# A two-layer hybrid diffusion step on one core: loads unpinned early, normalisation interleaved with gate products, attention paced closer

## The chip, the core and the metric

The kernel runs on one core of a Trainium2 chip. Its engines work side by side, each through a list of its own: TensorE (PE) multiplies matrices, VectorE (DVE), ScalarE (ACT) and GpSimd (POOL) do the elementwise work, and SyncE (SP) issues nearly all the transfers. A wait at the head of an engine's list holds back everything behind it on that engine. The metric is the device time of one execution in microseconds (us); lower is better.

## What is computed

The reference runs two layers. In each, 1024 latent tokens and 256 context tokens of width 1024 are normalised and modulated, go through one wide input projection, then through three token mixers (A, B and C), which are gated, merged and projected back:

```python
def mixer_inputs(x, cond, norm_g, w_ada, b_ada, w_in):
    mod = jax.nn.silu(cond) @ w_ada + b_ada
    ...
    shift, scale, gate = jnp.split(mod, 3, axis=-1)
    h = rms_norm(x, norm_g) * (1 + scale) + shift
    return jnp.split(h @ w_in, IN_OFFSETS, axis=-1), gate

def latent_layer(x, c, ka_c, va_c, kb_c, vb_c, st, ...):
    (aq, ak, av, ag, bq, bk, bv, bg, cx, cg, ga, gb, gc), gate = mixer_inputs(x, c, norm_g, w_ada, b_ada, w_in)
    ...
    ya = window_attention(qa, ka, va, ka_c, va_c, a_sink) * jax.nn.silu(ag)
    yb = neighbourhood_attention(qb, kb, vb, kb_c, vb_c, b_rpb) * jax.nn.silu(bg)
    ...
    yc = (hf + hb).astype(x.dtype) * jax.nn.silu(cg)
    out = merge_branches(ya, yb, yc, ga, gb, gc, w_br, w_out)
    return x + gate * out
```

The columns `ga`, `gb`, `gc` (1024 each) and `ag`, `bg`, `cg` (512 each) of the projection are gates: nothing needs them before the merge at the end of the layer. Mixer C is a linear recurrence over the tokens, behind a small convolution of `cx`. A and B are softmax attentions with 8 heads each; a latent query sees 512 cached keys and two or three blocks of 128 local ones.

## The kernel before

**Tiles.** Tokens stand in three chunks: 0 and 1 are the latent tokens (512 each), 2 is the context (256). Activations are kept as eight tiles of 128 features (k = 0 to 7), each split into a high and a low part (`hhl`/`hll` for the latent tokens, `hhc`/`hlc` for the context), and so are the weights. A product (`job`) makes 128 output columns of one chunk: 8 values of k with three matmuls each, high by high, low by high and high by low, so 24 matmuls of 512 or 256 columns.

**Weights.** `load_w` (L410) loads a job's weights in two halves into `wr` (two buffers); ACT casts each half to its high part (`wh`, four buffers), POOL subtracts for the low part (`wl`, four buffers). One job is loaded ahead of the one that runs (`Weave.fetch`, L137).

**The order.** The order on PE is written out by the program. `Weave` keeps a clock of its own, which each matmul advances, and two queues of jobs: `need` (what attention or the recurrence wait for) and `spare` (mostly the gates). Attention proceeds when its due times are reached, and a piece of a job (three matmuls) is put in wherever nothing is due. The other engines' lists come from a scheduler, which may move instructions by its own estimate. `ordered` (L210) holds the loads through it in program order while the list `starting` is not empty:

```python
def ordered(ins):
    return tc.keep_in_program_order(ins) if starting else ins
```

It is called on the loads of tokens (L1331), of weights (L414, L512), of the modulation (L1405) and on `keep` (L1355), which writes the transposed input to DRAM as `x_d`. A gate's way out is a copy on ACT into a tile `tgt` (L710) and a transfer from it into `g_d` (L711); these are not held.

**The first phase** (L1392 to L1471). Chunk 0 is transposed and normalised, then the gates of its columns 0 to 7 are made, then chunks 1 and 2 are transposed and their sums of squares taken. `fill(n)` puts in n pieces of gate jobs. `token_rstd` (two steps) makes the factors, and `norm_apply` normalises: per k a product on DVE (`nt`), an addition with a cast on ACT (`hhl`, L566) and a difference on DVE (`hll`, L567). The tiles `nt` and `tgt` share one tag, `g2`, with three buffers. In the traces `gt` is a gate product; in the order of instructions `gt_0_70` is the product for gate column 7 on chunk 0, and `wgt_0_70` its weights. After it comes `cx_0`, the first product of mixer C, on chunks 0, 1 and 2.

**Attention** (`chain`, L1079). A layer has 40 groups of 256 queries, in two steps each; a step scores two parts of 128 queries and one head (`sc` against the cached keys, `sl` against the local ones, both in PSUM tiles of tag `s`, of which there are two), and turns the probabilities of the step two before it (`pt`, `PT`) and multiplies them by the values (`o`). For one part DVE takes the minimum of `sc` (L981) and of both (L997), and ACT takes the exponentials (`P`, L1003 and L1005). A step starts no earlier than `pace` after the one before, on the clock of `Weave`, in ns:

```python
for s in range(2):
    yield max(g.q_at, g.keys.at["K"], paced)
    paced = W.now + T["pace"]
    yield from step(i, s, behind.popleft() if len(behind) == BEHIND else None)
```

The gate products that are left when attention ends run in the merge phase behind it. `sg` are the gate products of the mixers' own gates, the last in `spare`.

Of the kernel before, what the change touches and what calls it, by code (L numbers as in the profile page):

```python
# [76 lines left out]
PSB = {"d": 2, "s": 2, "t": 3, "o": 1}  # L77
LGB = ("s", "t")
LDB = ("d", "t")
T = dict(f1=9, f2=2, kc=10000, c0=10000, cq=1, gx=3, nx=8000, yo=1500, yi=1000, aq=9000, ac=7000, ms=2000, v=3200, tok=8600, scale=1100, t0=3400, tb=2200, o=2200, soft=7600, pace=9400, lg=320, lr=8500, cv=16000, le=4200)  # L80


class Weave:
# [107 lines left out]
def trunk(nc, tc, ctx, I, K, O):  # L191
# [20 lines left out]
    starting = [True]  # L212
# [28 lines left out]
    fill = cp.tile([P, 2], F32, name="fill")  # L241
# [304 lines left out]
    def sum_squares(l, ci, xs, acc, add):  # L546
        for k in range(KD):
            add_square(l, ci, k, xs[k][:, :CHUNKS[ci][1]], acc, add)
# [10 lines left out]
    def norm_apply(l, ci, xs, rs, H, ks=range(KD)):  # L559
        c0, N = CHUNKS[ci]  # L560
        cond = 0 if c0 < NLAT else 1
        for k in ks:
            t = cp.tile([P, 512], F32, tag="g2", name=f"nt{l}_{ci}_{k}", bufs=3)
            nc.vector.scalar_tensor_tensor(t[:, :N], xs[k][:, :N], hcol(l, k, cond), rs[:, :N], ALU.mult, ALU.mult)
            hh, hl = H.at(k, ci)
            nc.scalar.activation(hh, t[:, :N], AF.Identity, bias=scol(l, k, cond))  # L566
            nc.vector.scalar_tensor_tensor(hl, t[:, :N], scol(l, k, cond), f32(hh), ALU.add, ALU.subtract)  # L567
        W.mark(("H", l, ci), 6000)
# [813 lines left out]
    def fill(n):  # L1382
        for _ in range(n):
            W.dense()

    with tc.manual_schedule(engines={mybir.EngineType.PE}):
        sides = ("left", "right")
        hcm = pool("h0", side=sides[0])
        H = Hidden(hcm.__enter__(), 0)
        W.banks = ("d", "t")  # L1390
        jobs = gate_jobs(0, H)
        with pool("start", side=sides[1]) as sp:  # L1392
# [61 lines left out]
            xs.append(input_chunk(2, tk, sp))  # L1454
            acc.append(sp.tile([P, 512], F32, tag="nacc", name="nacc0_2", bufs=2))
            sum_squares(0, 2, xs[2], acc[2], nc.vector.tensor_add)
            fill(T["f1"])
            token_rstd(0, 1, acc[1])
            fill(T["f2"])
            token_rstd(0, 2, acc[2], "t", False)  # L1460
            norm_apply(0, 1, xs[1], acc[1], H)
            norm_apply(0, 2, xs[2], acc[2], H)
            for ci in (1, 2):
                for k in range(KD):
                    fill(1)
                    keep(ci, xs[ci], (k,))
                fill(1)
                if ci == 1:
                    constants(0)
            starting.clear()  # L1470
            bias_tables()  # L1471
        W.spare.extend((always, j((1, 2))) for j in jobs[:8])
        for l in range(DEPTH):
# [65 lines left out]
```

## Time and profile before

| what | value |
|---|---|
| median of 3 runs | 3178.77 us (3177.68 to 3180.86) |
| the profiled execution, its own time | 3178.1 us |
| its span in the profile | 3176.3 us |
| PE busy | 3081.1 us, 97% of the span |
| DVE, ACT, POOL busy | 1780.8, 1706.3, 969.8 us (56%, 54%, 31%) |
| 0 to 335 us | first phase and recurrence, layer 0 |
| 395 to 1290 us | attention, layer 0 |
| 1290 to 1990 us | merge, output, and the first part of layer 1 |
| 1990 to 2835 us | attention, layer 1 |
| 2835 to 3176 us | merge and output, layer 1 |

The busy time of an engine is the time in which one of its instructions was on. A matmul's record is longer than the distance to the next one, since matmuls overlap: rows at 0.39 us stand 0.23 us apart. Idle time of PE is listed with what ended it. The granted clock is TensorE's, as a share of 2.4 GHz; it has two levels, so a value between 0.5 and 1 for a stretch is a mean of both.

### The profile page before, as it was taken

Reading aid. Unit: us, or ns where it says so; the run is one execution under the profiler, and the core shown is the slowest. Engines: PE = TensorE matmul, PEld = TensorE weight load, DVE = VectorE, ACT = ScalarE, POOL = GpSimd, SP = SyncE. Lnnn points to the kernel's source line nnn. Section 1 sums busy time; section 2 is a strip of 40 time slices with the busy share of each in tenths; the row PEclk is TensorE's granted clock in tenths of the full one; section 3 lists DMA queues with packets and bytes.
Section 4 is the critical chain, followed back from the end, with each engine's and each line's share of the span. In section 5 each row is a group of like instructions: output and inputs, shape, how many; then the busy total and the mean of one; then the engine's idle time right before and its main releaser. Section 6 shows DMA issues by size and latency. Waiting matters only on the chain.

```text
span 3176.3 us, 48114 instructions
## 1 busy us (share of the span) xinstructions
PE 3081.1 (97%) x17421; PEld 2627.0 (83%) x17421; DVE 1780.8 (56%) x3293; ACT 1706.3 (54%) x3591; POOL 969.8 (31%) x815
## 2 busy tenths in 40 slices
PE   7799999999999999999999999999999999989999
PEld 5677788888888888888888888888888888878887
DVE  5475356666666664455364554665675666555531
ACT  5478355565555555444346864555555555544422
POOL 3364312223222120245343442222241222002632
PEclk9899999999999999999999999999999999989999
DMA  7554555535533232663442236455544333237443
GB/s 266 157 170 154 150 147 152 151 105 165 158 110 93 86 101 70 228 207 112 143 152 71 74 105 176 111 144 146 147 134 145 103 102 95 82 110 243 161 152 102
DMA packets 447434, 435.03 MB, mean 137 GB/s; under 512 B 75120, under 2 KB 368604, under 8 KB 445916
## 3 DMA queue, kind: packets, MB, share of 16 engines
q1 hardware_dynamic: 441212, 414.92, 43.9%
q0 software_dynamic: 5664, 16.83, 1.6%
q8 instruction: 137, 2.24, 0.3%
q14 instruction: 101, 0.83, 0.1%
q10 hardware_dynamic: 320, 0.21, 0.0%
HBM read 298.12 MB, written 137.29 MB: 137 GB/s over the span
## 4 chain that ended last, share of the span: by engine, by line
PE 78%; DVE 9%; ACT 5%; issue 3%; POOL 2%; DMA 2%; SPq 1%; ACTq 0%; DVEq 0%; POOLq 0%
PE gt L218 17%; PE sg L218 10%; PE o L218 7%; PE q L218 6%; PE pt L225 6%; PE po L218 5%; PE br L218 5%; PE k L218 4%; PE sc L218 4%; PE v L218 3%; PE cx L218 3%; PE sl L218 3%; POOL acc L1242 1%; PE lg L218 1%; DVE lR L687 1%
## 5 line engine op out<-in xcount | busy, mean ns | idle before, releaser
L427 ACT CAST PT<-pt 128x512 fp32r<-128x512 f32 (+2 forms) x528 | 271.7, 536 | 337.5 <-PE pt L225 335.4
L428 DVE TENSOR_TENSOR PT<-pt,PT 128x512 fp32r<-128x512 f32 (+2 forms) x528 | 319.5, 621 | 100.5 <-ACT PT L427 99.0
L981 DVE TENSOR_REDUCE st<-sc 128x1 f32<-128x512 f32 x256 | 176.3, 689 | 298.7 <-PE sc L218 298.2
L218 PE MATMUL gt<-hhl,wgt_h 128*128 128x512 f32 x736 | 299.7, 407 | 18.0 <-ACT wgt_h L422 18.0
L218 PE MATMUL gt<-hll,wgt_h 128*128 128x512 f32 x736 | 290.1, 394 | 0.0
L218 PE MATMUL gt<-hhl,wgt_l 128*128 128x512 f32 x736 | 289.9, 394 | 0.1
L225 PE MATMUL pt<-cst,P 128*128 128x128 f32 x1856 | 274.0, 274 | 9.4 <-DVE PT L428 7.5
L423 POOL TENSOR_TENSOR wgt_l<-wgt_r,wgt_h 128x512 fp32r<-128x512 f32 x110 | 173.0, 1580 | 335.6 <-ACT wgt_h L422 292.5
L225 PEld LDWEIGHTS pt<-cst,P 128*128 128x128 f32 x1856 | 217.7, 141 | 18.2 <-DVE PT L428 9.4
L218 PE MATMUL po<-z,wpo_h 128*128 128x512 f32 (+1 forms) x768 | 212.5, 364 | 7.7 <-ACT z L427 4.5
L1003 ACT ACTIVATE P<-sc,st 128x512 f32<-128x512 f32 x256 | 175.3, 685 | 61.7 <-DVE st L997 61.4
L218 PE MATMUL br<-yl,wbr_h 128*128 128x512 f32 (+1 forms) x576 | 205.2, 356 | 0.8 <-DVE yl L428 0.8
L218 PE MATMUL br<-yh,wbr_h 128*128 128x512 f32 (+1 forms) x576 | 204.7, 355 | 0.0
L218 PE MATMUL br<-yh,wbr_l 128*128 128x512 f32 (+1 forms) x576 | 204.5, 355 | 0.0
L423 POOL TENSOR_TENSOR wsg_l<-wsg_r,wsg_h 128x512 fp32r<-128x512 f32 x48 | 63.7, 1332 | 402.2 <-ACT wsg_h L422 398.4
L218 PE MATMUL sc<-Kpast,Q 128*128 128x512 f32 x512 | 168.4, 410 | 17.0 <-ACT P L1003 16.4
L218 PE MATMUL o<-PT,Vpast 128*128 128x256 f32 x1024 | 177.3, 295 | 3.7 <-DVE Y L1066 3.1
L218 PEld LDWEIGHTS gt<-hhl,wgt_h 128*128 128x128 f32 x736 | 138.8, 189 | 49.0 <-ACT wgt_h L422 18.4
L1005 ACT ACTIVATE P<-sl,st 128x384 f32<-128x384 f32 (+1 forms) x320 | 170.9, 534 | 4.6 <-DVE st L993 4.4
L218 PEld LDWEIGHTS gt<-hhl,wgt_l 128*128 128x128 f32 x736 | 138.5, 188 | 33.4 <-POOL wgt_l L423 1.2
L218 PEld LDWEIGHTS po<-z,wpo_h 128*128 128x128 f32 x768 | 137.1, 192 | 32.6 <-ACT z L427 5.8
L218 PEld LDWEIGHTS gt<-hll,wgt_h 128*128 128x128 f32 x736 | 139.0, 189 | 25.2 <-issue 0.5
(350 smaller groups left out, 8521.4 us busy)
## 6 DMA issues: line engine op xcount, KB each, us to landing
Q<-q_d SPq DMA_DIRECT2D x160, 256.0 KB
gl<-g_d SPq DMA_DIRECT2D x48, 640.0 KB
wgt_r<-in_w_in_dram SPq DMA_DIRECT2D x110, 256.0 KB
g_d<-tgt SPq DMA_DIRECT2D x92, 256.0 KB
wa<-in_w_ada_dram POOLq DMA_DIRECT2D x64, 256.0 KB, 4.2
wpo_r<-in_w_out_dram SPq DMA_DIRECT2D x64, 256.0 KB
yg<-y_d SPq DMA_DIRECT2D x24, 640.0 KB
yr<-s_d SPq DMA_DIRECT2D x24, 640.0 KB
```

The source lines that it names most:

```text
L218: nc.tensor.matmul(out, a, b, start=start, stop=stop)
L225: nc.tensor.transpose(out, x, idn)
L423: nc.gpsimd.tensor_sub(lo, r, f32(hi))
L427: nc.scalar.copy(hi, x)
L428: nc.vector.tensor_sub(lo, x, f32(hi))
L687: nc.vector.tensor_tensor_scan(h, a, u, st if c0 < NLAT else 0.0, ALU.mult, ALU.add)
L981: nc.vector.tensor_reduce(cm, psc, AX.X, ALU.min)
L1003: nc.scalar.activation(pt[:, nl * P:(nl + 4) * P], psc, AF.Exp, bias=m, scale=-1.0, accum_out=sums[:, t, x, 1:2])
L1005: nc.scalar.activation(pt[:, :nl * P], loc, AF.Exp, bias=m, scale=-1.0, accum_out=sums[:, t, x, 0:1])
L1242: (nc.vector if b == 0 and k >= KD - 2 else nc.gpsimd).tensor_add(z, z, g)
```

## The change

Three edits. The list `starting` is cleared ahead of `fill(T["f1"])`, so the loads and the `x_d` writes that come later in the program are no longer held in order. `norm_apply` for chunks 1 and 2 is called tile by tile between pieces of gate products, and `constants(0)` and the two calls of `keep` come behind them; the number of pieces is the same, 29. The due time between attention steps goes from 9400 to 9000.

```diff
-T = dict(f1=9, f2=2, ..., soft=7600, pace=9400, lg=320, lr=8500, cv=16000, le=4200)
+T = dict(f1=9, f2=2, ..., soft=7600, pace=9000, lg=320, lr=8500, cv=16000, le=4200)
...
             sum_squares(0, 2, xs[2], acc[2], nc.vector.tensor_add)
+            starting.clear()
             fill(T["f1"])
             token_rstd(0, 1, acc[1])
             fill(T["f2"])
             token_rstd(0, 2, acc[2], "t", False)
-            norm_apply(0, 1, xs[1], acc[1], H)
-            norm_apply(0, 2, xs[2], acc[2], H)
             for ci in (1, 2):
                 for k in range(KD):
+                    norm_apply(0, ci, xs[ci], acc[ci], H, (k,))
                     fill(1)
-                    keep(ci, xs[ci], (k,))
-                fill(1)
-                if ci == 1:
-                    constants(0)
-            starting.clear()
+            constants(0)
+            keep(1, xs[1])
+            keep(2, xs[2])
+            fill(2)
             bias_tables()
```

On SP, in the first phase, the row that matters is `g_d_0_5`, the way out of gate product 5, against the loads of `wgt_0_70`. Before:

```order
L1355 DMA x_d_6_78<-xi_6_719 128x512
L711 DMA g_d_0_5_117<-tgt_0_50_0_1035 128x512
L1355 DMA x_d_7_79<-xi_7_726 128x512
L414 DMA wgt_0_70_r_1074<-in_w_in_dram 128x4x128
L414 DMA wgt_0_70_r_1080<-in_w_in_dram 128x4x128
```

After, from the first load of `wgt_0_70` on, and then (second block) the stretch in which `g_d_0_5` stands now:

```order
L414 DMA wgt_0_70_r_995<-in_w_in_dram 128x4x128
L1355 DMA x_d_4_76<-xi_4_705 128x512
L1355 DMA x_d_5_77<-xi_5_712 128x512
L711 DMA g_d_0_4_116<-tgt_0_40_0_889 128x512
L414 DMA wgt_0_70_r_1001<-in_w_in_dram 128x4x128
```

```order
L414 DMA wcx_0_r_1140<-in_w_in_dram 128x4x128
L276 DMA sink_1229<-in_a_sink_dram 128x8
L414 DMA wgt_0_01_r_1174<-in_w_in_dram 128x4x128
L414 DMA wgt_0_01_r_1180<-in_w_in_dram 128x4x128
L414 DMA wgt_0_11_r_1298<-in_w_in_dram 128x4x128
L711 DMA g_d_0_5_117<-tgt_0_50_0_980 128x512
```

The loads of `wgt_0_70` moved ahead of `g_d_0_5`, and those of the three jobs behind it (`wcx_0`, `wgt_0_01`, half of `wgt_0_11`) too.

On ACT, in the same place, the casts of `wgt_0_70`, the copy `tgt_0_50` and the normalisation (`hhl`, `hhc`) share one list. Before:

```order
L566 ACTIVATE hhc_6_997<-nt_2_6_995,mod_222 128x256
L710 COPY tgt_0_50_0_1035<-gt_0_50_0_914 128x512
L710 COPY tgt_0_60_0_1119<-gt_0_60_0_1086 128x512
L566 ACTIVATE hhc_7_1003<-nt_2_7_1001,mod_222 128x256
L422 CAST wgt_0_70_0_h<-wgt_0_70_r_1074 128x512
L422 CAST wgt_0_70_4_h<-wgt_0_70_r_1080 128x512
```

After:

```order
L422 CAST wgt_0_70_0_h<-wgt_0_70_r_995 128x512
L533 ACTIVATE nw_1_895<-nacc_1_407 128x512
L533 ACTIVATE nw_2_920<-nacc_2_829 128x256
L422 CAST wgt_0_70_4_h<-wgt_0_70_r_1001 128x512
L566 ACTIVATE hhl_0_230<-nt_1_0_927,mod_222 128x512
L566 ACTIVATE hhl_1_232<-nt_1_1_934,mod_222 128x512
L566 ACTIVATE hhl_2_234<-nt_1_2_941,mod_222 128x512
L422 CAST wcx_0_0_h<-wcx_0_r_1134 128x512
```

The casts of `wgt_0_70` moved from behind the normalisation of chunks 1 and 2 to ahead of it, and those of `wcx_0` into it.

On PE, in attention, the pieces of gate products between two scores become fewer. This is the end of the first step of a group in layer 0 (the first group of the second head pair); `sc_1_0_1` is the first score of its second step. Before:

```order
L218 MATMUL gt_1_50_1_5007<-hhl_4_238,wgt_1_50_4_l 128x512
L218 MATMUL o_0_6_5025<-PT_0_6_0_2_5035,Vlat_0_3766 128x256 x4
L218 MATMUL o_0_6_5025<-PT_0_6_0_3_5044,Vlat_0_3766 128x128 x2
L218 MATMUL gt_1_50_1_5007<-hhl_5_240,wgt_1_50_4_h 128x512
L218 MATMUL gt_1_50_1_5007<-hll_5_241,wgt_1_50_4_h 128x512
L218 MATMUL gt_1_50_1_5007<-hhl_5_240,wgt_1_50_4_l 128x512
L218 MATMUL sc_1_0_1_5066<-Kpast_1_4885,Q_1_0_4666 128x512 x2
```

After:

```order
L218 MATMUL gt_1_50_1_5007<-hll_5_241,wgt_1_50_4_h 128x512
L218 MATMUL gt_1_50_1_5007<-hhl_5_240,wgt_1_50_4_l 128x512
L218 MATMUL o_0_6_5028<-PT_0_6_0_2_5038,Vlat_0_3766 128x256 x4
L218 MATMUL o_0_6_5028<-PT_0_6_0_3_5047,Vlat_0_3766 128x128 x2
L218 MATMUL sc_1_0_1_5066<-Kpast_1_4891,Q_1_0_4672 128x512 x2
```

The piece (three matmuls) that stood between `o` and the next step's first score is gone from this interval; the interval keeps three pieces ahead of `o`. Added up over the rows, 38400 columns of gate products, 75 matmuls of 512, leave the attention of layer 0 and run behind it.

On PE, at the end of layer 1's attention, the last score but one is followed by turns (`pt`) and the last score (`sc_3_6_3`). Before:

```order
L225 MATMUL pt_3_4_1_1_28678<-cst,P_3_4_3_28554 128x128
L218 MATMUL sc_3_6_3_28687<-Kpast_0_24268,Q_3_6_28417 128x512 x2
L218 MATMUL sl_3_6_3_28691<-Klat_0_24270,Q_3_6_28417 128x256 x2
L218 MATMUL o_3_4_28628<-PT_3_4_1_0_28675,Vpast_0_24552 128x256 x4
L225 MATMUL pt_3_4_1_2_28703<-cst,P_3_4_2_28515 128x128
```

After, from the last two pieces of twelve matmuls that now stand between `pt` and `sc`:

```order
L218 MATMUL sg_0_00_1_28595<-hhl_4_15412,wsg_0_00_4_h 128x512
L218 MATMUL sg_0_00_1_28595<-hll_4_15413,wsg_0_00_4_h 128x512
L218 MATMUL sg_0_00_1_28595<-hhl_4_15412,wsg_0_00_4_l 128x512
L218 MATMUL sg_0_00_1_28595<-hhl_5_15414,wsg_0_00_4_h 128x512
L218 MATMUL sg_0_00_1_28595<-hll_5_15415,wsg_0_00_4_h 128x512
L218 MATMUL sg_0_00_1_28595<-hhl_5_15414,wsg_0_00_4_l 128x512
L218 MATMUL sc_3_6_3_28650<-Kpast_0_24246,Q_3_6_28324 128x512 x2
L218 MATMUL sl_3_6_3_28654<-Klat_0_24248,Q_3_6_28324 128x256 x2
```

Before, no gate product stands between the last five scores or behind them until attention ends. After, 37632 columns (73.5 matmuls of 512) that stood in earlier steps of this layer's attention stand there: 28416 ahead of the last score (3072 of them ahead of the first of the five), 9216 behind it.

## Rows read from the trace of the kernel before

**Rows 1.** The page: busy us, share of the span and instructions of each engine.
```profile
PE 3081.1 (97%) x17421; PEld 2627.0 (83%) x17421; DVE 1780.8 (56%) x3293; ACT 1706.3 (54%) x3591; POOL 969.8 (31%) x815
```

**Rows 2.** PE in order of time, first phase: start us, length us; idle before it.
```profile
81.57 0.39 PE L218 MATMUL gt<-hhl,wgt_h 128*128 128x512 f32 x1
...
86.78 0.39 PE L218 MATMUL gt<-hhl,wgt_l 128*128 128x512 f32 x1
105.19 0.80 PE L218 MATMUL gt<-hhl,wgt_h 128*128 128x512 f32 x1 [18.02 <-ACT wgt_h L422]
...
112.88 0.39 PE L218 MATMUL cx<-hhl,wcx_h 128*128 128x512 f32 x1
```

**Rows 3.** SP's queue in order of time, the same stretch.
```profile
76.08 0.98 SPq L414 DMA_DIRECT2D wgt_r<-in_w_in_dram  x2
77.15 4.73 SPq L1355 DMA_DIRECT2D x_d<-xi  x7
100.38 0.32 SPq L711 DMA_DIRECT2D g_d<-tgt  x1
...
101.27 1.00 SPq L414 DMA_DIRECT2D wgt_r<-in_w_in_dram  x2
```

**Rows 4.** ACT in order of time: copies and casts ahead of PE's return.
```profile
99.77 1.07 ACT L710 COPY tgt<-gt 128x512 f32<-128x512 f32 x2 [0.33 <-DVE hlc L567]
...
104.52 0.62 ACT L422 CAST wgt_h<-wgt_r 128x512 fp32r<-128x512 f32 x1 [3.27 <-DMA wgt_r<-in_w_in_dram]
```

**Rows 5.** POOL in order of time: the low parts of gate job 6.
```profile
80.06 2.78 POOL L423 TENSOR_TENSOR wgt_l<-wgt_r,wgt_h 128x512 fp32r<-128x512 f32 x2 [4.49 <-ACT wgt_h L422]
```

**Rows 6.** DVE in order of time: last differences of chunk 1 and of chunk 2.
```profile
94.19 0.74 DVE L567 SCALAR_TENSOR_TENSOR hll<-nt,mod,hhl 128x512 fp32r<-128x512 f32 x1
...
101.28 0.48 DVE L567 SCALAR_TENSOR_TENSOR hlc<-nt,mod,hhc 128x256 fp32r<-128x256 f32 x1 [0.81 <-ACT hhc L566]
```

**Rows 7.** Stretch, busy us of PE, PEld, DVE, ACT, POOL, PE's clock, DMA share, GB/s.
```profile
105.00:113.00 8.00, 7.68 (x25) 5.77 (x26) 0.00 (x0) 1.38 (x3) 5.08 (x7) 0.74 0.94 303
2790.00:2815.00 25.00, 17.23 (x83) 14.44 (x81) 14.21 (x33) 12.25 (x34) 2.54 (x2) 0.73 0.14 43
2815.00:2835.00 20.00, 15.58 (x89) 12.97 (x90) 9.51 (x23) 8.23 (x22) 0.00 (x0) 0.91 0.02 7
```

**Rows 8.** The same view, four of the nine stretches of 5 us at attention's end.
```profile
2795.00:2800.00 5.00, 3.00 (x11) 2.33 (x11) 2.70 (x7) 3.31 (x10) 1.27 (x1) 0.55 0.45 131
2800.00:2805.00 5.00, 3.42 (x12) 2.73 (x12) 3.20 (x9) 2.44 (x8) 0.00 (x0) 0.50 0.08 27
2805.00:2810.00 5.00, 4.68 (x19) 4.29 (x19) 2.25 (x6) 1.85 (x6) 0.00 (x0) 0.59 0.01 3
...
2815.00:2820.00 5.00, 4.32 (x20) 3.96 (x20) 2.13 (x6) 2.33 (x9) 0.00 (x0) 0.66 0.00 0
```

**Rows 9.** PE in order of time, end of layer 1's attention.
```profile
2792.89 0.28 PE L218 MATMUL sg<-hhc,wsg_l 128*128 128x256 f32 x1
2795.01 0.85 PE L218 MATMUL sc<-Kpast,Q 128*128 128x512 f32 x2 [1.84 <-ACT P L1003]
...
2815.49 0.85 PE L218 MATMUL sc<-Kpast,Q 128*128 128x512 f32 x2 [2.08 <-ACT P L1003]
...
2833.02 0.48 PE L218 MATMUL sg<-hhl,wsg_h 128*128 128x512 f32 x1
```

**Rows 10.** PE and then ACT in order of time, a score inside layer 1's attention.
```profile
2678.37 0.71 PE L218 MATMUL sc<-Kpast,Q 128*128 128x512 f32 x2
...
2684.24 0.73 PE L218 MATMUL sc<-Kpast,Q 128*128 128x512 f32 x2 [0.88 <-ACT P L1003]
...
2683.42 0.67 ACT L1003 ACTIVATE P<-sc,st 128x512 f32<-128x512 f32 x1
```

**Rows 11.** PE's waits for a score's exponentials: layer 0's attention, then layer 1's until 2790 us.
```profile
PE sc L218 <- ACT P L1003: 5.0, 6, 1.1
PE sc L218 <- ACT P L1003: 3.9, 5, 1.0
```

## What the change is predicted to do

> **What bounds the kernel now.** I read the page first: PE is busy 97% of the span [rows 1], so the order of its work is worth what PE idles or runs slowly, 95 us of idling in all. The order of instructions shows the same matmuls before and after, only placed differently. So the question is which of PE's gaps the change closes, and which it opens. PE's waits in order of time show two places that stand out. The first is one wait of 18.02 us at 86.8 us, in the first phase [rows 2]. The second is the end of layer 1's attention, 2793 to 2833 us, where PE has no gate product left to put between the scores [rows 9]: 7.77 us idle ahead of the last score and 4.42 behind it (25 less 17.23, 20 less 15.58), at a granted clock of 0.73 and 0.91 [rows 7]. Inside attention PE waits 5.0 us in layer 0 and 3.9 in layer 1 for the exponentials of the score before [rows 11].
>
> **The first phase.** In SP's queue, seven `x_d` writes go out from 77.15 us, then `g_d` at 100.38 us [rows 3]; by the order that is `g_d_0_5`. It waits for the copy `tgt`, which ACT makes at 99.77 us, behind the normalisation of chunks 1 and 2 [rows 4]. The loads of `wgt_0_70` are behind it and go out at 101.27 us [rows 3], the cast begins at 104.52 [rows 4], and PE returns at 105.19 [rows 2]. So the wait is one of order, not of bandwidth.
>
> The change takes the loads out from behind `g_d_0_5`, and ACT's casts out from behind the normalisation. What PE gets back is 18.02 us and the slow restart: the 24 matmuls after the wait take 7.69 us (105.19 to 112.88), while the job before it takes 23 distances in 5.21 us (81.57 to 86.78), so 5.44 for 24 [rows 2]. That is 2.25 us, at a granted clock of 0.74 in that stretch [rows 7]. Together 20.3 us.
>
> What is late next? The weights first. A load can start when job 6's raw weights are converted, on POOL at 82.84 us at the times of before [rows 5]. From issue to cast 3.25 us pass (101.27 to 104.52) [rows 3, 4], the cast takes 0.62 [rows 4] and a subtraction 1.39 (half of 2.78) [rows 5]. That makes the low part ready at 88.1 us, where PE would want it at about 87.5, its third matmul: a wait of up to 0.7 us. The order puts job 6's casts earlier as well, so it may be nothing; I take 0.7 and count 19.6 us.
>
> Then the normalisation. PE would reach chunk 1 of `cx_0` at 97.9 us (87.0 and two jobs of 5.44) and chunk 2 at 103.3. DVE finishes chunk 1 at 94.93 and chunk 2 at 101.76 [rows 6]: 3.0 and 1.5 us to spare, and PE takes the eight tiles one after the other. The interleaving and the later `constants(0)` therefore cost nothing as long as this cover holds. The `x_d` writes keep their place behind the tokens and their queue; nobody reads `x_d` before the end of the layer. The two calls of `keep` issue the same 16 transfers as before. By the order, three kinds of small or later loads fall behind: the bias table and `sink` on SP go behind the `x_d` writes, and on POOL the loads of the modulation go behind four more subtractions, 5.6 us at 1.39 each [rows 5]. The first product that reads the modulation stands behind all of `cx_0`, two and a half jobs or 13.6 us, which hides that; if it didn't, 5.6 us would be the price.
>
> **Attention's end.** By the order, the shorter pace takes 37632 columns of gate products from earlier steps of layer 1 and leaves them for the end: 28416 ahead of the last score, 9216 behind it. A matmul of 512 columns costs 0.2265 us (5.21 over 23) [rows 2], so these are 12.6 and 4.1 us of work where PE idles now. Ahead of the last score I count the whole gap: 7.77 idle [rows 7] and what the low clock takes, which in the stretches at 0.55, 0.50 and 0.59 is 45, 50 and 41% of 3.00, 3.42 and 4.68 us [rows 8], 5.0 us together: 12.8 us. Behind it the gap is 4.42 idle and 34% of 4.32, 5.9 us [rows 7, 8]. The steps there are a chain through PE, ACT and DVE, and the last turns have no gate product between them in the order, so I count half, 2.9. That makes 15.7 us.
>
> Layer 0's attention has no such end; there 38400 columns (75 matmuls, 17 us) only move behind attention, at the same price.
>
> **What the shorter pace costs.** A score may begin when ACT has taken the exponential of the one before: from a score's start at 2678.37 us to the end of `P` at 2684.09 it is 5.72 us, and the next score follows at 2684.24 after a wait of 0.88 us [rows 10]. Such waits exist now, 11 in the two attentions [rows 11], so a shorter distance between scores comes back as a wait wherever the chain is already the longer. I did this for each of the 230 pairs of successive latent scores: the distance in PE's rows, less the time to the end of `P` in ACT's and 0.14 us of handing over, less what the order takes out of that interval at 0.2275 us per 512 columns. In the pair of [rows 10] the order takes out 1.0 us and all of it returns. In 14 pairs something returns, 0.1 to 1.0 us each, 3.6 us in layer 0 and 3.3 in layer 1: 6.9 us. The bounds are nothing, if DVE and ACT get their work sooner too, and 33.8 us, if every one of the 148.5 matmuls taken out of the steps returns as a wait. I take 6.9, since the order says where the distances shrink and the rows say where they can.
>
> The Trainium skill's "Perfetto Trace Analysis", section Optimization Strategy, says of a gap that repeats on the engine that should be saturated that it can mean too little SBUF or PSUM for the next tile. The waits of [rows 11] are of that kind, behind two tiles of tag `s`; by that rule alone, which speaks against the closer pace, these waits would grow with every step, and the sum would go to the third rival's.
>
> **The sum.** 19.6 + 15.7 - 6.9 = 28.4 us. The profiled execution took 3178.1 us, which gives 3149.7; the median of the runs is 0.7 us above it, so I put it at 3150.
>
> **Rivals.** (1) The first phase's wait is replaced. ACT's list now has the casts of `wcx_0` and `wgt_0_01` between the additions of the normalisation, and a cast whose load has not landed holds up `hhl` behind it. If three casts each wait a full load of 3.25 us, the normalisation is 9.8 us later, 6.8 beyond its 3.0 to spare: 3157 us. For it: the DMA queue also carries the `x_d` writes there. Against it: by the order each load is issued a job ahead.
>
> (2) Attention's end stays slow: the gaps of the last steps are filled only in part, the clock falls there all the same, and only the 7.8 us of idling ahead of the last score come back, 7.9 less than counted: 3158 us. The Trainium skill's "TensorE: Matmul & The Clock Gate", section What's actually happening, says that the slow clock is the default and activity lifts it; by that rule the last steps, which keep gaps behind the last score, could pay it again. In the rows the clock fell to 0.55 right after the gate products ended [rows 8, 9].
>
> (3) The scores become the bound in all of attention: the chain through DVE and ACT, not the pace, sets the step, and all 33.8 us come back as waits: 3178.8 - 35.3 + 33.8 = 3177 us, no difference. (4) The same with a further price, slower than before: DVE and ACT serve scores and turns in one list, and as steps come closer a score's minimum stands behind a turn. At 0.3 us more per step, a third of the wait of [rows 10], the 160 steps cost 48 us: 3178.8 - 35.3 + 48 = 3191.5. It decides from 0.26 us a step (35.3 and 6.4 over 160). Against both: 11 waits in some 1600 us of attention [rows 11], and the order shortens mostly the longer one of a step's two intervals. (5) The changed order does nothing for the first wait, because another transfer in SP's queue stands in front of the loads: without that term, 3170.
>
> **Chances.** Forecast 0.66, with a range of its own of 3143 to 3157; (1) 0.13, (2) 0.12, (3) 0.03, (4) 0.03, (5) 0.03. The range reaches from 20.3 and 18.6 us gained with nothing lost (3178.8 - 38.9 = 3140) to beyond rivals 1 and 2 (3157, 3158), with a little for both in part: 3139 to 3162. A measurement of this kernel tells about 0.2%, 6.4 us, from no change. Faster by more: the forecast and rivals 1, 2 and 5, 0.94. Within: rival 3, 0.03. Slower: rival 4, 0.03.
>
> **What would show it.** Right: no wait of PE over 2 us after `gt_0_60`, the loads of job 7 issued before 85 us, the clock at 1.00 from 90 to 130 us; PE busy over 90% ahead of attention's last score; the waits for `P` in attention between 9 and 20 us in sum. Wrong: a new wait at `cx_0` behind a cast (1), a clock near 0.5 at the last steps (2), or waits for `P` beyond 30 us (3, 4).

## The result and the profile after

The changed kernel takes 3152.23 us (median of 4 runs, 3148.27 to 3155.3), the kernel before beside it 3178.22 (4 runs, 3173.28 to 3180.86): a ratio of 0.9919, 95% interval 0.9901 to 0.9938. The prediction was 3150. The profiled execution took 3155.3 us, with a span of 3153.5, which is 22.8 below the 3176.3 of before; it is the slowest of the four, so the account below is of 22.8 us, where the medians differ by 26.0.

On the page of the changed kernel PE is no busier in microseconds than in [rows 1] (3080.7 against 3081.1); the gain is idle time that is gone.

```profile
PE 3080.7 (98%) x17421; PEld 2629.2 (83%) x17421; DVE 1786.2 (57%) x3293; ACT 1708.8 (54%) x3591; POOL 971.1 (31%) x815
```

**The first phase**, against [rows 3]. SP's queue after: the two loads of gate job 7 go out at 77.56 and 80.25 us, among the writes of `x_d` and no longer behind them.

```profile
77.56 0.38 SPq L414 DMA_DIRECT2D wgt_r<-in_w_in_dram  x1
78.04 0.93 SPq L1355 DMA_DIRECT2D x_d<-xi  x2
...
80.25 0.38 SPq L414 DMA_DIRECT2D wgt_r<-in_w_in_dram  x1
80.72 6.78 SPq L1355 DMA_DIRECT2D x_d<-xi  x10
```

ACT's list after, against [rows 4]: job 7's cast is done by 85.61 us, ahead of the normalisation, and two later casts wait for their loads between the additions, 1.72 and 2.24 us. That is how rival 1 begins.

```profile
84.99 0.62 ACT L422 CAST wgt_h<-wgt_r 128x512 fp32r<-128x512 f32 x1 [1.11 <-PE gt L218]
87.83 2.05 ACT L566 ACTIVATE hhl<-nt,mod 128x512 fp32r<-128x512 f32 x3 [2.21 <-DVE nt L564]
91.60 0.62 ACT L422 CAST wcx_h<-wcx_r 128x512 fp32r<-128x512 f32 x1 [1.72 <-DMA wcx_r<-in_w_in_dram]
...
97.14 0.63 ACT L422 CAST wgt_h<-wgt_r 128x512 fp32r<-128x512 f32 x1 [2.24 <-DMA wgt_r<-in_w_in_dram]
97.67 0.58 ACT L710 COPY tgt<-gt 128x512 f32<-128x512 f32 x1
```

By stretches (columns as in [rows 7]): from 87 to 113 us, where before PE waited 18.02 us and restarted at 0.74, it is busy 25.75 of 26 us at a clock of 1.00. The 25 us that end just behind the last score (at 2792.7 us) are full, and in the 16 us behind them 1.59 us are idle.

```profile
87.00:113.00 26.00, 25.75 (x123) 21.49 (x122) 21.84 (x40) 14.98 (x28) 10.61 (x11) 1.00 0.45 141
...
2770.00:2795.00 25.00, 25.00 (x154) 22.16 (x153) 13.84 (x37) 14.82 (x42) 2.58 (x2) 1.00 0.16 54
2795.00:2811.00 16.00, 14.41 (x100) 12.65 (x99) 8.84 (x18) 8.57 (x21) 2.55 (x2) 1.00 0.21 66
```

**Inside attention**, against [rows 11]. PE's waits after, layer 0's attention and then layer 1's up to 2778 us (what for: us, times, longest): the waits for `P` stand at 4.6 and 4.4, as before (5.0 and 3.9). The waits of other kinds have changed places: for the square of a query (`q_sq`) 3.0 us instead of 1.2, and for the copies of keys (`ko`) and values (`vr`) 2.1 and 1.5, where before had 3.8 for `PT` and 1.3 for `k_sq`.

```profile
PE sc L218 <- ACT P L1003: 4.6, 6, 1.2
PE q_ms L218 <- ACT q_sq L736: 3.0, 1, 3.0
PE pt L225 <- ACT ko L810: 2.1, 1, 2.1
PE vt L225 <- ACT vr L830: 1.5, 1, 1.5
...
PE sc L218 <- ACT P L1003: 4.4, 7, 1.2
PE q_ms L218 <- ACT q_sq L736: 2.9, 1, 2.9
```

Two of the waits before, in layer 0's attention:

```profile
PE pt L225 <- DVE PT L428: 3.8, 4, 2.6
...
PE q_ms L218 <- ACT q_sq L736: 1.2, 1, 1.2
```

**Where the 22.8 us arise.** Every kernel here runs the same matmuls, so each one's start can be set against its start before. The table has the difference at eight of them, in us (negative: earlier), in the profiled execution of each kernel. The times at the head are those of before: the sum of squares of chunk 2 (76), the first matmul of `cx_0` (113) and its 53rd, in chunk 2 (125), a product of keys (360), the first matmul of layer 0's merge (1332), layer 1's normalisation (1630), layer 1's merge (2890), the last output (3169).

| kernel | 76 | 113 | 125 | 360 | 1332 | 1630 | 2890 | 3169 |
|---|---|---|---|---|---|---|---|---|
| changed, first profile | 3.4 | -17.0 | -17.8 | -12.2 | -4.4 | -6.4 | -23.9 | -22.8 |
| changed, again | 1.6 | -18.8 | -19.7 | -10.0 | -2.2 | -4.2 | -21.9 | -20.5 |
| pace alone | -1.1 | -0.9 | 0.4 | -0.8 | 3.9 | 0.9 | -16.4 | -15.0 |
| first phase alone | -0.4 | -20.8 | -21.6 | -15.4 | -15.4 | -14.8 | -18.5 | -18.6 |
| unpinned alone | -0.3 | -20.7 | -12.7 | -8.6 | -8.6 | -7.7 | -6.3 | -6.0 |
| interleaved alone | -0.9 | -2.9 | -0.8 | 2.4 | 2.5 | 1.0 | 0.6 | 1.7 |
| unpinned, other banks | 0.4 | -20.0 | -20.9 | -8.0 | -8.0 | -7.3 | -6.2 | -7.2 |
| pace 9000 in layer 1 alone | 0.1 | -20.3 | -21.1 | -14.5 | -14.4 | -16.5 | -33.2 | -34.1 |
| pace 8600 | -0.2 | -20.6 | -21.5 | -15.7 | -12.7 | -14.2 | -36.1 | -33.2 |
| pace 8000 | -0.3 | -20.7 | -21.5 | -14.9 | -4.2 | -3.3 | -14.3 | -14.3 |
| 9400 and 8600 | 1.5 | -19.0 | -19.8 | -12.5 | -9.3 | -11.5 | -33.3 | -33.2 |
| 9800 and 8600 | 1.7 | -18.8 | -19.6 | -12.3 | -13.9 | -11.2 | -32.2 | -32.8 |

In the first row: 3.4 us lost ahead of 76 us, 20.4 gained between 76 and 113, 5.6 given back between 125 and 360, 7.8 lost in layer 0's attention, 2.0 regained behind it, 17.5 gained in layer 1's attention.

### The profile page after: what moved, and what is told of

Same layout as the page of the kernel before. It is cut to its first block, busy times and chain, and to the rows that moved or that the text cites. A ratio compares the mean times of both kernels' runs of the same rounds, so it can differ in the third digit from the quotient of the medians.

```text
span 3153.5 us, 48110 instructions
## 1 busy us (share of the span) xinstructions
PE 3080.7 (98%) x17421; PEld 2629.2 (83%) x17421; DVE 1786.2 (57%) x3293; ACT 1708.8 (54%) x3591; POOL 971.1 (31%) x815
## 3 DMA queue, kind: packets, MB, share of 16 engines
q8 instruction: 137, 2.24, 0.3%
## 4 chain that ended last, share of the span: by engine, by line
PE 64%; DVE 6%; POOL 3%; ACT 2%; issue 2%; DMA 2%; SPq 0%; ACTq 0%; POOLq 0%; DVEq 0%
PE gt L218 14%; PE sg L218 10%; PE br L218 6%; PE o L218 5%; PE po L218 5%; PE pt L225 5%; PE q L218 4%; PE sc L218 3%; PE k L218 3%; PE v L218 2%; PE sl L218 2%; PE cx L218 2%; POOL acc L1242 1%; PE lg L218 1%; DVE gl L1241 1%
## 5 line engine op out<-in xcount | busy, mean ns | idle before, releaser
L1005 ACT ACTIVATE P<-sl,st 128x384 f32<-128x384 f32 (+1 forms) x320 | 170.7, 533 | 17.6 <-DVE st L993 17.3
```

The lines of the kernel that those rows point to most:

```text
L1005: nc.scalar.activation(pt[:, :nl * P], loc, AF.Exp, bias=m, scale=-1.0, accum_out=sums[:, t, x, 0:1])
```

## The experiments

### The pace alone

```diff
-  ... pace=9400 ...
+  ... pace=9000 ...
```

> The kernel before with the pace of 9000 alone. Theory (the three edits act apart, by stage): layer 0's attention loses 3.6 us by the prediction and 7.8 by the changed kernel's trace, layer 1's gains 12.4 by the prediction and 17.5 by the trace, the work moved between the two attentions is neutral to 2 us. So 8.8 us faster by the prediction's terms, 10.6 by the trace's: ratio 0.9967 to 0.9973, with the 18 us wait of the first phase still there at 86.8 us. Rival (the pace did nothing, all of the gain is the first phase): ratio 0.999 to 1.001. Rival (the closer pace is a loss that the first phase hid): ratio above 1.002.

Measured: 3166.31 us, ratio 0.9961 (0.9946 to 0.9977), a little more than the theory's 0.9967 to 0.9973, which the interval holds. Both rivals fall. Layer 0's attention lost 4.7 us (from -0.8 to 3.9 in the table), of which 3.0 came back behind it, and layer 1's gained 17.3 (0.9 to -16.4).

### The first phase alone

```diff
-  ... pace=9000 ...
+  ... pace=9400 ...
```

(from the changed kernel)

> The changed kernel with the pace of 9400 put back, so the first phase's two edits alone. Theory (the first phase's gain stays until the end): 19.6 us faster, ratio 0.9938. Second theory (part of it is given back in the recurrence, where the changed kernel's lead fell from 17.8 us at 123 us to 12.1 at 341 us, and in the first 76 us, where it lost 3.4): 12 to 15 us faster, ratio 0.9953 to 0.9962. If the lead at 341 us is again near 12 us, the giving back belongs to the first phase's edits and not to chance; if the lead at 76 us is near 0 instead of -3.4, the loss there was chance.

Measured: 3160.91 us, ratio 0.9948 (0.9933 to 0.9962), 15.6 us faster by the medians: between the two theories, and the interval does not tell them apart. The trace does: of a lead of 21.6 us at 125 us, 6.2 are given back by 360 us, as in the changed kernel (5.6), so the giving back belongs to the first phase's edits. The lead at 360 us is 15.4 and not near 12, because the 3.4 us lost ahead of 76 us are not lost here (0.4 gained); so those are no part of the change. The two experiments add up to the change within their intervals: 0.39% and 0.52% against 0.81%.

This kernel also gains 3.7 us at the end of layer 1's attention (1630 to 2890), where its order is that of before. Its windows there have the low clock in one stretch of 5 us only, the one below, where before had four ([rows 8]); so part of what the low clock costs there differs from one execution to the next. Five of the profiles have this order on PE in layer 1. In the 45 us around attention's end their granted clock is 0.81 (before), 0.96 (here), 0.85 (unpinned alone) and twice 0.77 (interleaved alone, other banks): this kernel is the exception.

```profile
2780.00:2785.00 5.00, 3.08 (x10) 2.47 (x10) 2.55 (x7) 3.08 (x10) 1.28 (x1) 0.66 0.42 121
```

### Unpinned alone, interleaved alone

From the kernel before, unpinned alone:

```diff
+            starting.clear()
             fill(T["f1"])
...
-            starting.clear()
             bias_tables()
```

> Only the pins taken off early: the normalisation and the tokens' writes are called as in the kernel before, pace 9400. Theory (the wait of 18 us is a matter of the order in which loads, casts and the copy of the gate stand in their queues, and the pins hold that order): in the order of this kernel the loads of gate job 7 stand ahead of g_d_0_5 and their casts ahead of the normalisation, so the wait at 86.8 us falls below 2 us without any interleaving: 16 to 20 us faster at 123 us, 12 to 20 in all, ratio 0.994 to 0.996. Rival (it takes the interleaving to let the casts through): the wait stays above 8 us, ratio above 0.997.

From the kernel before, interleaved alone:

```diff
-            norm_apply(0, 1, xs[1], acc[1], H)
-            norm_apply(0, 2, xs[2], acc[2], H)
...
+                    norm_apply(0, ci, xs[ci], acc[ci], H, (k,))
                     fill(1)
-                    keep(ci, xs[ci], (k,))
...
+            constants(0)
+            keep(1, xs[1])
+            keep(2, xs[2])
+            fill(2)
             starting.clear()
```

> Only the interleaving of normalisation and gate products, with the pins kept to the end of the phase, pace 9400. Theory: in the order of this kernel the copy that g_d_0_5 waits for stands behind the seventh addition of chunk 1 (91.92 us before) instead of behind chunk 2's (99.77), the loads follow at about 94 and the casts at about 98, so the wait shrinks from 18.0 us to 10 or 11 and does not go away: 7 to 9 us faster at 123 us, ratio 0.997 to 0.998. Rival (the interleaving is what closes the wait): wait below 2 us, ratio 0.994 to 0.996.

Measured: unpinned alone 3170.89 us, ratio 0.9978 (0.9968 to 0.9988); interleaved alone 3183.47, ratio 1.0016 (1.0007 to 1.0025), a little slower than before. By the medians they are worth 15.6 us together, apart 5.6 and -6.9. So neither theory held as it was put.

Unpinned alone, the 18 us wait is gone, as expected. But PE in order of time shows a wait of 7.00 us between the first chunk of `cx_0` and the second, for a copy `tgt`, and ACT's list shows that copy behind the additions of chunk 2.

```profile
97.36 0.39 PE L218 MATMUL cx<-hhl,wcx_l 128*128 128x512 f32 x1
104.75 0.79 PE L218 MATMUL cx<-hhl,wcx_h 128*128 128x512 f32 x1 [7.00 <-ACT tgt L710]
...
102.53 1.31 ACT L566 ACTIVATE hhc<-nt,mod 128x256 fp32r<-128x256 f32 x3 [1.07 <-DVE nt L564]
104.11 1.07 ACT L710 COPY tgt<-gt 128x512 f32<-128x512 f32 x2 [0.28 <-DVE hlc L567]
```

Interleaved alone, the first wait shrinks to 10.18 us, as expected, and `cx_0` then waits 4.90 us for its own weights, whose loads the pins still hold. The two rows of PE:

```profile
96.44 0.79 PE L218 MATMUL gt<-hhl,wgt_h 128*128 128x512 f32 x1 [10.18 <-ACT wgt_h L422]
...
109.96 0.79 PE L218 MATMUL cx<-hhl,wcx_h 128*128 128x512 f32 x1 [4.90 <-ACT wcx_h L422]
```

### Unpinned, with other banks

What is left of the wait in the unpinned kernel could be a PSUM bank: by the order in which the tags rotate, the second chunk of `cx_0` takes the bank of gate job 5's product. The edit gives the first phase's last gate jobs the tags `s` and `t` instead of `d` and `t`:

```diff
             starting.clear()
+            W.banks = ("s", "t")
```

> The kernel with only the pins taken off early, and the gate jobs of the first phase put into the banks of tags s and t instead of d and t; the order of the instructions of the first phase is the same as in that kernel. Theory (its 7.0 us wait at the second chunk of cx_0 is for a bank: gate job 5's product still lies in the bank that cx_0_1 needs, and its copy stands on ACT behind the normalisation of chunk 2): with another bank for job 5 the wait falls below 1.5 us, and the lead at 125 us rises from 12.7 to 18 to 20.5 us, as much as with the interleaving; ratio 0.994 to 0.996. Rival (the chunk itself is late, behind ACT's casts): the wait stays at 5 to 7 us under another name, and the ratio at 0.998.

Measured: 3171.69 us, ratio 0.9984 (0.9975 to 0.9993). PE's only wait from 80 to 125 us is 0.84 us, and the copies on ACT are as late as ever:

```profile
108.22 0.50 PE L218 MATMUL gt<-hhl,wgt_h 128*128 128x512 f32 x1 [0.84 <-ACT tgt L710]
...
104.82 1.07 ACT L710 COPY tgt<-gt 128x512 f32<-128x512 f32 x2 [0.27 <-DVE hlc L567]
```

So the wait was for the bank, and the lead at 125 us is 20.9, as with the interleaving. That part of the theory held, but the ratio did not: between 125 and 360 us this kernel gives back 12.9 us, and ends where the unpinned one does. So the bank is the cause of the wait, but not of the whole difference to the interleaving: with the pins off, the interleaved versions still have 10.0 to 15.7 us of lead at 360 us, the two versions without interleaving 8.0 and 8.6. The interleaved kernel with the pins loses 3.2 us in the same stretch, with hardly a lead to give back (0.8). What sets the limit there is not shown.

### The closer pace in layer 1 alone, and the changed kernel again

```diff
-                    paced = W.now + T["pace"]
+                    paced = W.now + (T["pace"] if l else 9400)
```

> The changed kernel with the closer pace in layer 1 alone (layer 0 keeps 9400). Theory: the closer pace pays only where attention ends without gate products, in layer 1; in layer 0 it costs 4.7 us of attention by the run with the pace alone and 7.8 by the changed kernel's profile, of which 2 to 3 come back behind it. So 2 to 6 us faster than the changed kernel: 3146 to 3151 us, ratio to the kernel before 0.990 to 0.992; the waits for the key and value copies and the squares of the queries at 783, 811 and 907 us are gone from layer 0. Rival (layer 0's price is chance of the clock): within 1 us of the changed kernel, ratio 0.992 to 0.994.

> The changed kernel again, beside the two versions above on the same chip. It tells what of its first profile was chance: 3.4 us lost by 76 us, which no other run with the same start shows, and clocks below 0.9 in four stretches of layer 0's attention. Theory (chance): the loss by 76 us is below 1 us, the lead at 360 us is 14 to 16 us, and the span is 2 to 5 us below the first profile's 3153.5. Rival (they belong to the change): 3 to 4 us lost by 76 us again.

Measured: in layer 1 alone 3144.74 us, ratio 0.9897 (0.9882 to 0.9912); the changed kernel again 3153.69, ratio 0.9929 (0.9915 to 0.9943). These two intervals do not overlap; that of the change's first measurement (0.9901 to 0.9938) overlaps a little with the first. The traces bear it out that layer 0's closer pace costs time. With the order of 9400, layer 0's attention took 930.7 to 930.8 us in six profiles and 933.9 in a seventh; with that of 9000 it took 935.4 (the pace alone), 938.5 and 938.5. The version with 9000 in layer 1 alone is also faster than the 3146 to 3151 expected, and the waits at 783, 811 and 907 us are gone from layer 0, as expected. Layer 0's attention as one window (first score to first matmul of the merge), in the kernel before, the changed kernel (the second profile of it has 938.54 us, 924.51 busy), and with the closer pace in layer 1 alone:

```profile
400.87:1331.59 930.72, 917.63 (x5538) 805.52 (x5537) 570.09 (x1224) 531.27 (x1344) 212.07 (x189) 1.00 0.44 130
```

```profile
388.66:1327.17 938.51, 924.57 (x5538) 810.85 (x5537) 568.40 (x1224) 533.74 (x1344) 214.10 (x189) 0.99 0.44 129
```

```profile
386.36:1317.14 930.78, 917.70 (x5538) 805.59 (x5537) 570.49 (x1224) 530.39 (x1343) 211.71 (x188) 1.00 0.44 130
```

The stretch is 7.8 us longer, in both profiles, with the same matmuls: 0.85 us more idle (13.94 against 13.09), and 6.9 more of busy time, nearly all because the clock fell. It falls at the waits that changed places: at 907 us PE waits 3.04 us for a `q_sq` that stands on ACT behind a score's exponentials, and the two stretches of 5 us at its end have a clock of 0.67 and 0.65. In windows of 10 us the clock is 0.83, 0.83, 0.90 and 0.76 behind the waits at 783, 811 and 907 us and above 0.97 in all others, which is 6.8 us of 40. The changed kernel's second profile has them at the same places. With the pace alone, where the same waits come at other moments, the clock fell once, at 917 us, over two windows, and layer 0 lost 4.7 (1.8 of it idle). Before, where the waits add up to nearly as much, the clock did not fall in this stretch.

```profile
906.86 0.38 ACT L736 ACTIVATE q_sq<-q 128x256 f32<-128x256 f32 x1
...
907.29 1.22 PE L218 MATMUL q_ms<-q_sq,cst 128*128 128x256 f32 x2 [3.04 <-ACT q_sq L736]
...
905.00:910.00 5.00, 2.71 (x7) 2.33 (x8) 3.30 (x7) 2.24 (x7) 0.00 (x0) 0.67 0.53 162
910.00:915.00 5.00, 5.00 (x19) 4.12 (x18) 2.12 (x7) 2.25 (x7) 4.03 (x4) 0.65 0.00 0
```

The Trainium skill's "TensorE: Matmul & The Clock Gate", section What's actually happening, says that activity is what lifts the slow clock; the rows agree: from 910 us on PE is busy throughout, and from 915 us the clock is 1.00 again. Here the slow stretches cost several times what the waits add.

As to chance: the loss by 76 us was 1.6 us in the second profile and 1.5 and 1.7 in its two neighbours on that chip, between 1.1 gained and 0.4 lost elsewhere. So it goes with the run and not with the change, though the 1 us that I had set as the bound was too tight. The clock accounts for it: over the same matmuls up to 76 us it is 0.93 before and 0.89 in the first profile, with as much idling (15.89 and 15.60 us).

```profile
0.00:76.36 76.36, 60.47 (x305) 41.62 (x306) 43.72 (x105) 39.22 (x73) 25.15 (x33) 0.93 0.78 266
```

```profile
0.00:79.77 79.77, 64.17 (x305) 44.65 (x306) 44.85 (x105) 39.97 (x75) 26.87 (x35) 0.89 0.82 276
```

The rest of that expectation failed: the lead at 360 us is 10.0 and not 14 to 16, and the span, 3155.8, is 2.3 us above the first profile's instead of 2 to 5 below it. The low clocks in layer 0, which it took for chance, came again at the same places.

### Closer still: 8600 and 8000

```diff
-  ... pace=9000 ...
+  ... pace=8600 ...     (and, in a second kernel, pace=8000)
```

> The changed kernel with the pace set to 8600: 12288 more columns of gate products (24 matmuls, 5.5 us) leave each layer's attention. Theory (a shorter distance is not a wait as long as DVE and ACT are less than fully busy): PE's waits for P stay between 8 and 13 us in sum, and the time is within 4 us of the changed kernel, since layer 1's end has only 1.6 us of idle left to fill. Third rival of the prediction (the chain sets the step): all of the 11 us come back as waits for P, 11 us slower than the changed kernel. Fourth rival (0.3 us more for each of 160 steps): 48 us slower.

> The changed kernel with the pace set to 8000: 49152 more columns (96 matmuls, 21.8 us) leave each layer's attention. Theory (the prediction's pricing, by which a pair of scores returns what falls below its chain of some 5.9 us): many pairs now reach the chain, and a third to two thirds of 43.6 us come back as waits for P: 15 to 29 us slower than the changed kernel, waits for P between 22 and 40 us. If nothing comes back (below 5 us), the chain shortens with the pace and the price per pair has no ground at all. Third rival: all of it comes back, 44 us slower, about 3196 us.

Measured: 8600 takes 3146.08 us, ratio 0.9905 (0.9890 to 0.9920), some 6 us below the change's 3152.23 where within 4 was expected, but the intervals overlap; 8000 takes 3166.65, ratio 0.9965 (0.9952 to 0.9977), some 14 us slower, just under the 15 to 29 expected. PE's waits for `P` in sum, at 8600 and at 8000 (the whole kernel; at these paces all but 0.3 us of them lie inside the two attentions ahead of their ends):

```profile
PE sc L218 <- ACT P L1003: 16.4, 14, 3.1
```

```profile
PE sc L218 <- ACT P L1003: 23.4, 26, 1.9
```

At 9400 they were 8.9 inside attention, at 9000 9.0. So the price in score waits begins below 9000; at 8000 14.4 us of the 43.6 taken out come back in them, a third, the low end of what was expected. Rivals 3 and 4 of the prediction did not come true at any of these paces. At 8600 the waits reached 16.4, above the 8 to 13 of the theory, and layer 1's attention still gained 21.9 us against 17.5 at 9000. Layer 0's lost 7.8 at 9000, 3.0 at 8600 and 10.7 at 8000 (360 to 1332): its price does not follow the pace step by step. Nor is it the clock each time. At 8000 the clock stays at 1.00 in layer 0's attention; 4.3 of the 10.7 us are idle (17.43 against 13.09), and the other 6.4 are busy time over the same matmuls, which nothing here explains.

```profile
385.98:1327.42 941.44, 924.01 (x5539) 804.36 (x5537) 570.78 (x1224) 533.44 (x1344) 215.04 (x189) 1.00 0.44 129
```

### Two versions put together

Layer 0 at 9400 and layer 1 at 8600; and layer 0 at 9800, layer 1 at 8600:

```diff
-                    paced = W.now + T["pace"]
+                    paced = W.now + (T["pace"] if l else 9400)      (and 9800)
-  ... pace=9000 ...
+  ... pace=8600 ...
```

> The first phase as changed, layer 0's pace 9400, layer 1's 8600. Theory (the closer pace pays at layer 1's end alone, and there still at 8600): layer 0 as in the run with the closer pace in layer 1 alone (16.5 us ahead of before at 1630 us), layer 1 as in the run with 8600 in both (22 us more until attention's end, 3.4 back behind it): 35 us faster than before, 3140 to 3144 us, ratio 0.988 to 0.990. Rival (the 22 us hold only because layer 0 runs at 8600 too): not faster than 3145.

> As the run with 9400 and 8600, but layer 0's pace 9800: 36864 columns (72 matmuls, 16.4 us) that run behind layer 0's attention stand between its scores instead. Theory (layer 0's attention loses by waits whose number falls with the distance): the 5 us of waits for P in layer 0 fall to 1 to 4, and the time is 0 to 3 us below the run with 9400. Rival (waits in layer 0 come from where ACT's list puts the squares and copies of q, k and v, not from the distance): other waits take their place, within 1.5 us either way or up to 4 slower.

Measured: 3144.20 us, ratio 0.9896 (0.9882 to 0.9909), and 3146.69, ratio 0.9909 (0.9892 to 0.9926). The first beats the changed kernel beside it (0.9929, 0.9915 to 0.9943) with intervals apart, by some 9 us, but not the version with 9000 in layer 1 alone (0.9897): in the profiles 8600 gains 5.1 us more in layer 1, and loses 1.4 ahead of 76 us and 3.1 in layer 0's attention, where PE's order is the same in both. So whether 8600 is better than 9000 in layer 1 is not shown. A wider pace in layer 0 does shorten its attention (1.6 us gained from 360 to 1332), but 2.7 are lost behind it, so 9400 may as well stay. That is the rival's case: the waits for `P` in layer 0 fell to 2.9, as the theory had it, others took their place, and the kernel is 2.5 us slower by the medians, which the intervals do not tell from none.

The version with 9400 and 8600 shows one thing more. Its order on PE in layer 0 is that of the version with 9000 in layer 1 alone, and so are its waits: one of 2.6 us for `PT` early in attention, one of 1.3 for `k_sq`. Yet its layer 0 lost 3.2 us (360 to 1332), the other's 0.1. Behind those two waits the clock of its 10 us windows is 0.84 and 0.86; in the other it stays above 0.97 throughout.

## Why the prediction was right

**The first phase: right in size, the parts wrong.** 20.3 us were worked out and 19.6 counted; the trace shows 20.4 between 76 and 113 us, no wait at job 7's weights and a clock of 1.00. The 0.7 us for late weights was not needed. But the prediction gave all of it to the loads and the casts, and said of the interleaving that it costs nothing while its cover holds. It did not ask what ACT's copies of the gates do for PE. Taken alone the unpinning loses 8.0 of its 20.4 us again to a bank whose copy stands behind the normalisation; the interleaving is what brings that copy forward, from 104.11 to 97.67 us (94.02 in the first phase alone, which reaches 76 us as early as the unpinned kernel). The Trainium skill's "Perfetto Trace Analysis", section Matmuls, advises rotating independent products through different banks, so that one is emptied while the next runs; the bank experiment agrees (7.00 us to none). In the unpinned kernel the products rotate too, but there the copy comes only after three more products, and PE waits for it.

**Not in the sum: the recurrence.** Between 125 and 360 us the lead shrinks by 5.6 us. No step of the prediction looked there, except for the cover of the modulation. PE's longest waits in that stretch, before and then after (over the same matmuls; 8.0 and 12.1 us in all):

```profile
PE k L218 <- ACT wk_h L422: 1.8, 1, 1.8
PE k L218 <- POOL wk_l L423: 1.7, 1, 1.7
PE lg L218 <- ACT lJ L646: 1.5, 1, 1.5
...
PE lg L218 <- DVE mod L363: 0.9, 1, 0.9
```

```profile
PE k L218 <- ACT wk_h L422: 3.0, 1, 3.0
PE lg L218 <- DVE mod L363: 2.7, 1, 2.7
PE lg L218 <- POOL gl L613: 1.5, 1, 1.5
PE gt L218 <- ACT wgt_h L422: 1.3, 1, 1.3
```

They are longer and of more kinds, for weights and for results of the recurrence on DVE, ACT and POOL. All interleaved versions with the pins off give back 5.6 to 9.7 us there, and the one with other banks 12.9. Most of the 5.6 us is that idling (4.1 us more), the rest the clock (0.99 and 0.98 over the stretch). Which of these chains sets the limit was not tried and stays open.

**Attention's end: right.** The prediction counted 15.7 us less a price of 3.3, 12.4 for layer 1; the trace shows 17.5, 17.7 and 17.3 in the three kernels with 9000 in both layers, 16.7 with 9000 in layer 1 alone. In the 75 us around attention's end PE is busy 62.82 us before and 73.41 after:

```profile
2770.00:2845.00 75.00, 62.82 (x335) 53.13 (x334) 34.84 (x80) 34.19 (x87) 5.07 (x4) 0.89 0.25 81
```

```profile
2756.00:2831.00 75.00, 73.41 (x422) 63.29 (x421) 38.65 (x77) 39.26 (x90) 9.76 (x7) 1.00 0.38 124
```

That is 10.6 us of idling, and with the 6.5 that the low clock took in [rows 8] 17.1. Two terms were off: only half of the 5.9 us behind the last score was counted, and nearly all came back, and the price in layer 1 did not arise. The 6.5 us of clock are in part chance: four of the five profiles with that order have the low clock there, the first phase alone hardly.

**The price of the closer pace: the step that failed.** The pricing took the chain of each pair of scores as fixed, and what the order took out of the distance as coming back. It put 6.9 us on waits for `P`; these went from 8.9 to 9.0. The pair of [rows 10] is the plainest case. After, its second score follows 4.43 us after the first instead of 5.87, with no wait, because the exponential ends 3.88 us after the score's start instead of 5.72:

```profile
2661.78 0.63 PE L218 MATMUL sc<-Kpast,Q 128*128 128x512 f32 x2
...
2666.21 0.63 PE L218 MATMUL sc<-Kpast,Q 128*128 128x512 f32 x2
...
2664.99 0.67 ACT L1003 ACTIVATE P<-sc,st 128x512 f32<-128x512 f32 x1
```

The reason stands in DVE's list. In the kernel before, DVE is at work on a query when the score is done, and its minimum of the score begins 1.97 us after the score's start; in the changed kernel it begins 0.67 us after it:

```profile
2680.34 0.69 DVE L981 TENSOR_REDUCE st<-sc 128x1 f32<-128x512 f32 x1
```

```profile
2662.45 0.69 DVE L981 TENSOR_REDUCE st<-sc 128x1 f32<-128x512 f32 x1
```

So this chain is as long as what else stands in the lists of DVE and ACT at that moment, and the closer pace moves that too: the mean over all 256 scores is 3.66 us before and 3.71 after, but the long ones are at other places. The lower bound of the prediction, nothing, was the right one for this term. What the pace did cost is 7.8 us in layer 0, and 4.7 in the run with the pace alone, whose order on PE in layer 0 is the same. Of the 7.8, 0.85 are idling and the rest mostly the low clock at the waits on `ko`, `vr` and `q_sq`. Before had waits of that size there (2.6 us for `PT`) with no low clock, so no row of it showed this price. The 2.0 us that come back behind layer 0's attention come with the clock as well: it is 0.66 from 1510 to 1520 us before, and 1.00 from 1505 to 1515 after. That the net price, 5.8 us, lies near the 6.9 of the sum is luck: it arose in layer 0 alone, and by another mechanism.

**The rivals.** (1) ACT's casts wait between the additions, but for 1.72 and 2.24 us, not 9.8 in sum, and `cx_0` shows no wait. (2) The clock stays at 1.00 at attention's end. (3), (4) and (5) fell. The signs that were to show the prediction right came, the last one only at its edge: the waits for `P` were 9.0 us, of 9 to 20, without the 6.9 that were to be added to them.

**The sum** was 28.4 us, and 22.8 came: 5.1 more in layer 1, against 5.6 given back in the recurrence, 2.2 more net in layer 0 (5.8 against 3.6) and the 3.4 ahead of 76 us that go with the run. These leave 22.3; 1.6 more in the first phase (up to 125 us) and 1.1 less behind 2890 us make up the rest. The time was close because these nearly cancel, not because each was known.

## What to carry to other kernels

Where an order of loads is loosened and a wait closes, look at what the engine meets next, and above all at which PSUM bank it wants and where the copy that empties it stands: the loosening and the interleaving here were worth 15.6 us together, and 5.6 and -6.9 apart. A rate that is set for a whole loop is best set where it pays: the closer pace gained 17 us in the layer whose attention ran out of filler and lost 2 to 6, net of what came back, at that same pace in the one that did not. A chain measured in one order is no constant of the other order.

## What the runs showed of the hardware

Waits of 1.5 to 3 us in a PE that is otherwise full were followed by stretches at the lower clock: after the wait of 3.04 us for `q_sq`, 5 us at 0.65 in one profile of the changed kernel and at 0.50, the lower of its two levels (1.2 of 2.4 GHz), in the other. In layer 0 busy time rose by 6.9 us where the idling itself rose by 0.85. It does not follow on every such wait: the same wait for `PT`, in the same order, was followed by the lower clock in one profile (2.62 us) and not in the other (2.63):

```profile
473.84 0.66 PE L225 MATMUL pt<-cst,P 128*128 128x128 f32 x4 [2.62 <-DVE PT L428]
```

```profile
471.87 0.66 PE L225 MATMUL pt<-cst,P 128*128 128x128 f32 x4 [2.63 <-DVE PT L428]
```

So a single profile's difference of 2 or 3 us in a stage with such waits says little. A table of waits does not show it; a table of the granted clock by windows does.
